# Nine selections beside the chunked phases, stores from GpSimd's own queue, and shorter rings of K and V

## The chip, the cores and the metric

The kernel runs on one core of one Trainium2 chip. The metric is the device time of one execution in microseconds (us). A core has five engines that each take their instructions in order: TensorE (PE in the profile; PEld are its weight loads), VectorE (DVE), ScalarE (ACT), GpSimd (POOL) and SyncE (SP), which issues most DMA transfers.

## The reference, cut to what matters

Two blocks follow each other on 2048 tokens of width 1024, in float32. The first (sliding-window attention, a gated recurrence, a mixture of experts) is not touched. The second is:

```
xn   = rms_norm(h, gain);  proj = xn @ w_in
qa, ka, va, ga, qb, kb, vb, gb, iq, ik, iw, za, zb = split(proj)
ya = chunked_relpos_attention(qa, ka, va, rel_bias) * silu(ga)
yb = dsa_sparse_attention(rope(qb), rope(kb), vb, rope(iq), rope(ik), iw) * silu(gb)
merged = sigmoid(za + b0) * (ya @ w_branch_a) + sigmoid(zb + b1) * (yb @ w_branch_b)
out = rms_norm(h + merged @ w_out, final_gain)
```

In the chunked attention, each chunk of 64 queries sees its own 64 keys and the 512 before them, in 8 heads of 64. In the sparse attention, each block of 128 queries (16 blocks) first selects keys: 8 index heads of 32 give `score = sum_h relu(iq_h . ik) * iw_h` over all keys up to the block's end, and each query keeps the 256 keys of highest score. Softmax attention of 8 heads with one shared key and value head of 64 then runs over the kept keys.

## The kernel before, in words

The second block is class `S3`. Products that need full precision are done as three products of a high and a low part (`mm3`); the parts have names ending in h and l, or `whi`, `wlo`.

**Who sets the order.** The program is written by generators ("lanes") that a small planner interleaves (`B.run`). Each lane yields until the engine that it wants, and its operands, are ready by the planner's own clock (`Clock`, `Engine.cost`); then its instruction is written down. Front lanes come first; the lane in `back` (named `fill`) gets an engine only when no front lane wants it. The result is a fixed order for each engine, which the chip follows; waits are semaphores.

**The phases** (`run`, from L2858 on):

- *Norms.* `norm_lane` gathers expert results (`cy`, by indirect DMA from GpSimd), adds (`cx`), normalises, transposes. `proj(0, ...)` begins the projections of the first 1024 tokens (half 0). `ev_n` copies a result out of PSUM; queries of the sparse part and of the index are rotated on GpSimd (`rotate`) and stored by SP to DRAM tensors QB and IQ.
- *Chunked phase 0* (`chunked(0, ...)`): 32 units `a_unit(p, c, t)`, for a pair of heads p and a block of 128 queries. K and V come in blocks of 256 tokens through a ring of `KR` = 6 blocks (`k_lane`); a unit uses three of them. Scores `pS<-K,Q`, bias and maximum on VectorE (`sc`), exponential on ScalarE, division by the sum on GpSimd (`softmax`: `sc<-sc,ast`), transposes `pT<-ident,sc` on PE, split (`split_p`, `pp`), products `pU<-pp,V`. Then GpSimd multiplies by the gate (`gate`: `ot<-ot,sg`), and the product is stored to YT by SP. The rest of the projections of half 0 and the start of half 1 is the `fill`.
- *Sparse phase 0* (`sparse(range(SPLIT), ...)`, SPLIT = 10): blocks 0 to 9. For each block `sel_unit` makes the selection: 8 index heads by pieces of 512 keys (`pS<-ikS,iqs`), relu on ScalarE (`rl<-pS`), accumulation on VectorE (`acc<-rl,iw,acc`), then `search`: 12 steps of bisection for the threshold, each a pass of ScalarE over the row (`bias<-acc,sst`) and two tiny ones (`sst<-sst`), and some passes of VectorE. The result is a row of biases, 0 or a large negative number (`bias`). Then 4 units `b_unit(blk, p)` do the attention: scores `pS<-kbS,qd`, `scb`, transposes `pT<-ident,scb`, products `pU<-pp,vbS`, gate, store to YT.
- *Chunked phase 1* with the last projections of half 1 as fill, then the rest of them.
- *Sparse phase 1*: blocks 10 to 15, with `tail(c)` as fill: for each 256 tokens the branch projections (`pA<-yt,..`, `pA<-yh,..`), the merge gates (`tz`), the output projection (`pA<-..,mh`, `pA<-..,ml`), the final norm. `tail(c)` loads YT of blocks 2c and 2c + 1, all heads, so it can start only when their sparse units are done; the last, `tail(7)`, needs block 15. ScalarE and VectorE split what it loads (`yh<-yt`, `yt<-yt,yh`).

`bias_load` and the DRAM tensor BIAS exist already: a selection in `stored` writes its row there, and a sparse phase loads it in place of making it. Before, nothing was stored. In `chunked`, `sel` sets how many buffers there are:

```
self.P, self.nrb, self.nsel, self.nrl, self.npp = P, 1 if sel else 2, 1, 1 if sel else 2, 2 if half and sel else 3
self.NM = (max(sel, default=0) + 1) * 128
self.stored.update(sel)
```

Of the kernel before, what the change touches and what calls it, by code (L numbers as in the profile page):

```python
# [103 lines left out]
class Engine:  # L104
# [11 lines left out]
    def __getattr__(self, f):  # L116
        real = getattr(self.eng, f)
        if not callable(real) or f in ("preload_act_table_set",):
            return real

        def call(*a, **k):
            r = real(*a, **k)  # L122
            out = k.get("out", a[0] if a else None)
            if is_ap(out):
                outs = [out] + [k[x] for x in ("accum_out",) if is_ap(k.get(x))]
                ins = [x for x in a[0 if "out" in k else 1:] if is_ap(x)]
                ins += [x for y, x in k.items() if y not in ("out", "accum_out") and is_ap(x)]
                ins += [x.ap for x in k.values() if hasattr(x, "ap") and not is_ap(x) and is_ap(x.ap)]
                cost, lat = self.cost(f, out, ins, k, [x for x in a + tuple(k.values()) if isinstance(x, AF)])
                self.clock.op(self.name, outs, ins, cost, lat, 1.46 if f == "indirect_dma_start" else 0.0)  # L130
            return r
        return call

    def cost(self, f, out, ins, k, fs):
        n = out.free_size()
        if f in ("dma_start", "indirect_dma_start"):
            b = out.size() * 4 if callable(out.size) else out.size * 4
            return (1.04, 0.0) if f != "dma_start" else (b / 3.6e5, 0.0)
        if self.name == "tensor":
# [1714 lines left out]
SPLIT = 10  # L1854
KR = 6


class S3:
# [190 lines left out]

    def store(self, dst, t, src=None, key=None):  # L2050

        b = self.b
        yield from b.on("sync", t)
        self.nc.sync.dma_start(dst, t.bitcast(F32) if src is None else src)
        b.done(t)
# [4 lines left out]
    def ev_n(self, g, blk, ps):  # L2060
# [14 lines left out]
        elif g:  # L2075
# [13 lines left out]
            yield 1  # L2089
            yield from self.store(dst, x, x.rearrange("p h d -> p (h d)"), key)  # L2090
        else:
# [109 lines left out]
    def k_lane(self, half):  # L2201

        b, nc, P, c = self.b, self.nc, self.P, self.b.clock
        self.K = P.tile([128, 2, 256 * KR], F32R, name="K", bufs=1)
# [50 lines left out]
    def a_unit(self, p, c, t):  # L2255
# [10 lines left out]
        place = lambda kt: ring[(blk - 4 + kt) // 2][0] * 2 + (blk + kt) % 2  # L2266
        r0, end = place(kts[0]) * 128, 256 * KR
        q_ = slice(t * 128, t * 128 + 128)
# [127 lines left out]
    def gate(self, ot, g, i, blk):  # L2396
# [3 lines left out]
        b.done(g)  # L2400
        yield from self.store(self.YT[i, :, blk * 128:blk * 128 + 128], ot, None, ("y", i, blk))

# [438 lines left out]
    def run(self):  # L2841
# [18 lines left out]
        with self.b.pool("s_k") as c:  # L2860
            self.consts(c)
            self.keys(c)
            with ExitStack() as st:
                en = lambda name: st.enter_context(b.pool(name))
                b.nld = 1
                self.XN, self.ld, Wp, self.st = en("s_xn"), en("s_ld"), en("s_w"), en("s_st")
                self.W = Weights(b, self.ld, Wp, srcs, ring=3, ahead=1, store=self.parts, keep=dict(enumerate(order)))
                b.lanes = [self.weight_lane()]
                with b.pool("s_ro") as c:
                    self.rope = c.tile([128, NTB, 24], F32, name="rope")  # L2870
                    with b.pool("s_c") as self.C:
# [7 lines left out]
                    self.W.hi_eng = "gpsimd"  # L2879
                    self.chunked(0, fill, ())  # L2880
                    self.sparse(range(SPLIT), fill)
                    self.go(fill)
                fill = chain(self.keep(), self.proj(1, range(12, 32), last=True))
                self.chunked(1, fill, ())
                self.go(fill)
# [54 lines left out]
    def chunked(self, half, fill, sel):  # L2940

        with self.b.pool("s_a") as P:
            self.P, self.nrb, self.nsel, self.nrl, self.npp = P, 1 if sel else 2, 1, 1 if sel else 2, 2 if half and sel else 3
            self.NM = (max(sel, default=0) + 1) * 128
# [150 lines left out]
```

## Time and profile before

| what | value |
|---|---|
| median of 3 runs | 4131.68 us (4124.09 to 4132.37) |
| profiled execution, its own time | 4132.75 us |
| its span, first to last instruction | 4131.0 us |
| mean granted TensorE clock | 0.944 of full speed |
| busy share of the span: PE / VectorE / ScalarE / GpSimd | 89 / 66 / 55 / 19% |
| second block in that span | from about 1645 us to the end |
| chunked phase 0 / sparse phase 0 / chunked phase 1 / tails and sparse phase 1 begin at about | 2018 / 2330 / 2957 / 3304 us |

Durations are from the profiled execution. An engine's busy time leaves out waits; PE's matmuls overlap, so 100% busy says that one follows another without a gap, and the granted clock says at which of its two levels (1.2 or 2.4 GHz) they ran. "Idle before, releaser" names what ended an engine's wait.

### The profile page before, as it was taken

The page shows a single profiled execution, that of the slowest core. Times are in us where ns is not written, and L with a number is a line of the kernel's source. Part 1 is how long each engine was busy: PE and PEld are TensorE (multiplying, and loading weights), DVE is VectorE, ACT ScalarE, POOL GpSimd, SP SyncE. Part 2 cuts the span into 40 slices and gives each one's busy share as a digit, 9 for nine tenths or more (in the row PEclk, how much of TensorE's full clock was granted, in tenths as well). Part 3 has the DMA queues.
Part 4 walks back from the last instruction along what each step waited for, and adds up shares of the span by engine and source line. Part 5 has one row for each costly group of instructions (what it writes and reads, how often), then busy time and mean ns, then how long its engine had stood idle before and what let it go on. Part 6 is the DMA issues. An engine that isn't in the chain of part 4 may idle for free.

```text
span 4131.0 us, 64766 instructions
## 1 busy us (share of the span) xinstructions
PE 3675.2 (89%) x21649; PEld 3189.6 (77%) x21649; DVE 2738.2 (66%) x7027; ACT 2265.0 (55%) x4628; POOL 788.6 (19%) x1474
## 2 busy tenths in 40 slices
PE   3999999979969998488899989999799979999796
PEld 2888788768858887487788879988588868988686
DVE  7866875688877776744356556775566148888772
ACT  3644654555546665433234468874355248767851
POOL 1310000131011110561144324100133111111000
PEclk9999999979989999699999989999799989999897
DMA  6232441134368886768888753443466398876155
GB/s 222 80 115 98 161 168 72 54 116 148 123 235 316 317 307 242 265 233 303 258 267 265 225 191 102 130 129 130 122 177 171 111 305 292 308 264 232 48 180 186
DMA packets 442096, 792.24 MB, mean 192 GB/s; under 512 B 129072, under 2 KB 267280, under 8 KB 440848
## 3 DMA queue, kind: packets, MB, share of 16 engines
q1 hardware_dynamic: 430224, 754.35, 54.1%
q0 software_dynamic: 11520, 33.57, 2.5%
q8 instruction: 176, 2.88, 0.3%
q14 instruction: 176, 1.44, 0.1%
HBM read 566.50 MB, written 229.65 MB: 193 GB/s over the span
## 4 chain that ended last, share of the span: by engine, by line
PE 35%; DMA 6%; DVE 5%; issue 4%; ACT 2%; SPq 1%; POOL 1%; DVEq 0%; POOLq 0%; ACTq 0%
PE pA L122 22%; PE pS L122 5%; PE pT L122 4%; PE pU L122 4%; DMA tz<-TZ 2%; DMA x<-IQ 1%; SPq L122 1%; DVE acc L122 1%; DVE pp L122 1%; DVE scb L122 1%; DMA x<-QB 0%; ACT bias L122 0%; ACT pp L122 0%; DMA V<-VA 0%; DMA Q<-QA 0%
## 5 line engine op out<-in xcount | busy, mean ns | idle before, releaser
L122 PE MATMUL pA<-xnl,whi 128*128 128x512 f32 x1024 | 412.8, 403 | 0.0
L122 DVE TENSOR_TENSOR wlo<-ld,whi 128x1024 fp32r<-128x1024 f32 x271 | 327.1, 1237 | 114.2 <-ACT whi L122 56.6
L122 PE MATMUL pA<-xnh,whi 128*128 128x512 f32 x1024 | 402.2, 393 | 0.0
L122 PE MATMUL pA<-xnh,wlo 128*128 128x512 f32 x1024 | 401.9, 392 | 0.0
L122 DVE TENSOR_TENSOR pp<-pT,pp 128x256 fp32r<-128x256 f32 (+1 forms) x568 | 296.5, 539 | 134.3 <-ACT pp L122 129.7
L122 ACT ACTIVATE pp<-pT 128x256 fp32r<-128x256 f32 (+1 forms) x568 | 261.1, 478 | 226.5 <-PE pT L122 214.7
L122 PE MATMUL pA<-hlo,whi 128*128 128x512 f32 x832 | 352.4, 424 | 10.0 <-issue 6.6
L122 PE MATMUL pA<-hhi,wlo 128*128 128x512 f32 x832 | 329.7, 396 | 0.0
L122 PE MATMUL pA<-hhi,whi 128*128 128x512 f32 x832 | 328.8, 395 | 0.0
L122 ACT ACTIVATE whi<-ld 128x1024 fp32r<-128x1024 f32 x212 | 213.2, 1052 | 50.4 <-PE pA L122 35.0
L122 DVE SCALAR_TENSOR_TENSOR acc<-rl,iw,acc 128x512 f32<-128x512 f32 (+3 forms) x304 | 213.6, 703 | 37.0 <-ACT rl L122 24.0
L122 PE MATMUL pU<-pp,vbS 128*128 128x256 f32 x1088 | 212.7, 309 | 21.3 <-DVE pp L122 13.5
L122 PEld LDWEIGHTS pA<-xnh,wlo 128*128 128x128 f32 x1024 | 193.1, 189 | 42.8
L122 PE MATMUL pA<-wlo,xnh 128*128 128x256 f32 (+1 forms) x672 | 203.8, 303 | 25.1 <-DMA xnh<-XND 6.8
L122 ACT ACTIVATE bias<-acc,sst 128x384 f32<-128x384 f32 (+13 forms) x168 | 219.8, 1309 | 8.7 <-DVE sst L122 6.2
L122 PEld LDWEIGHTS pA<-xnl,whi 128*128 128x128 f32 x1024 | 194.0, 189 | 30.8
L122 PEld LDWEIGHTS pA<-xnh,whi 128*128 128x128 f32 x1024 | 193.8, 189 | 30.6
L122 PE MATMUL pA<-whi,xnl 128*128 128x256 f32 (+1 forms) x672 | 198.9, 296 | 4.0 <-DMA xnl<-XND 4.0
L122 PE MATMUL pA<-whi,xnh 128*128 128x256 f32 (+1 forms) x672 | 198.9, 296 | 0.0
L122 PEld LDWEIGHTS pU<-pp,vbS 128*128 128x128 f32 x1088 | 165.5, 199 | 37.5 <-DVE pp L122 21.2
L122 PE MATMUL pS<-kbS,qd 128*128 128x512 f32 (+3 forms) x640 | 183.0, 385 | 9.9 <-DVE bst L122 6.6
L122 ACT ACTIVATE rl<-pS 128x512 f32<-128x512 f32 (+3 forms) x304 | 159.3, 542 | 58.0 <-PE pS L122 29.7
(491 smaller groups left out, 10917.4 us busy)
## 6 DMA issues: line engine op xcount, KB each, us to landing
whi<-W2P SPq DMA_DIRECT2D x172, 512.0 KB
wlo<-W2P SPq DMA_DIRECT2D x172, 512.0 KB
ld<-in_w_gu_dram SPq DMA_DIRECT2D x128, 512.0 KB
ld<-in_w_dn_dram SPq DMA_DIRECT2D x64, 512.0 KB
W2P<-whi SPq DMA_DIRECT2D x57, 512.0 KB
W2P<-wlo SPq DMA_DIRECT2D x57, 512.0 KB
Y<-ym SPq DMA_DIRECT2D x48, 512.0 KB
xl<-in_wadaT_dram SPq DMA_DIRECT2D x32, 512.0 KB
```

The lines of the kernel that those rows point to most:

```text
L122: r = real(*a, **k)
```

## The change

1. The selections of blocks 2 to 7 run as a front lane beside chunked phase 0, those of blocks 10 to 12 beside chunked phase 1. Their bias rows go to BIAS, and the sparse phases load them. Blocks 0, 1, 8, 9 and 13 to 15 stay where they were. With selections beside it, a chunked phase has one `rl`, one `acc`, 4 in place of 5 rows `sc`, and in half 1 two products `pp` in place of three.
2. Stores of what GpSimd has written last (YT after the gate, QB and IQ after the rotation) are issued by GpSimd's queue instead of SP's: 128 + 32 + 16. The planner counts 1.04 us of GpSimd for one, and the bytes on the DMA engines.
3. The ring of K and V has 4 blocks in half 0 and 5 in half 1, instead of 6. The buffer into which raw weights are loaded lies in a pool that ends with sparse phase 0.

```diff
@@ Engine.__getattr__, Engine.cost @@
-                self.clock.op(self.name, outs, ins, cost, lat, 1.46 if f == "indirect_dma_start" else 0.0)
+                far = 1.46 if f == "indirect_dma_start" else out.size() * 4 / 3.6e5 if f == "dma_start" and self.name != "sync" else 0.0
+                self.clock.op(self.name, outs, ins, cost, lat, far)
...
-            return (1.04, 0.0) if f != "dma_start" else (b / 3.6e5, 0.0)
+            return (1.04, 0.0) if f != "dma_start" or self.name != "sync" else (b / 3.6e5, 0.0)
@@ S3 @@
-KR = 6
...
-    def store(self, dst, t, src=None, key=None):
+    def store(self, dst, t, src=None, key=None, eng="sync"):
...
-        yield from b.on("sync", t)
-        self.nc.sync.dma_start(dst, t.bitcast(F32) if src is None else src)
+        yield from b.on(eng, t)
+        getattr(self.nc, eng).dma_start(dst, t.bitcast(F32) if src is None else src)
@@ ev_n @@
-            yield from self.store(dst, x, x.rearrange("p h d -> p (h d)"), key)
+            yield from self.store(dst, x, x.rearrange("p h d -> p (h d)"), key, "gpsimd")
@@ gate @@
-        yield from self.store(self.YT[i, :, blk * 128:blk * 128 + 128], ot, None, ("y", i, blk))
+        yield from self.store(self.YT[i, :, blk * 128:blk * 128 + 128], ot, None, ("y", i, blk), "gpsimd")
@@ run @@
-                self.XN, self.ld, Wp, self.st = en("s_xn"), en("s_ld"), en("s_w"), en("s_st")
-                self.W = Weights(b, self.ld, Wp, srcs, ring=3, ahead=1, store=self.parts, keep=dict(enumerate(order)))
-                b.lanes = [self.weight_lane()]
+                self.XN, Wp, self.st = en("s_xn"), en("s_w"), en("s_st")
+
                 with b.pool("s_ro") as c:
+                    self.W = Weights(b, c, Wp, srcs, ring=3, ahead=1, store=self.parts, keep=dict(enumerate(order)))
+                    b.lanes = [self.weight_lane()]
...
-                    self.chunked(0, fill, ())
+
+                    self.chunked(0, fill, range(2, 8))
...
-                self.chunked(1, fill, ())
+                self.chunked(1, fill, range(SPLIT, SPLIT + 3))
@@ chunked @@
-            self.P, self.nrb, self.nsel, self.nrl, self.npp = P, 1 if sel else 2, 1, 1 if sel else 2, 2 if half and sel else 3
+            self.KR = 4 + half
+            self.P, self.nrb, self.nsel, self.nrl, self.npp = P, 2, 1, 1 if sel else 2, 2 if half and sel else 3
```

The order of the instructions moves at three places. On PE, at the end of sparse phase 1, around the last product of block 15 (`pU<-pp,vbS`; tiles carry the number that the program gave them), the kernel before has:

```order
L122 MATMUL pT_45846<-ident,scb_45546 128x128
L122 MATMUL pU_45752<-pp_45840,vbS 128x256 x4
L122 MATMUL pU_45752<-pp_45851,vbS 128x256 x2
L122 MATMUL pU_45752<-ident,rr_45859 128x128
L122 MATMUL pU_45752<-pp_45851,vbS 128x256 x2
L122 MATMUL pA_45885<-yt_45876,whi_45312 128x256
L122 MATMUL pA_45885<-yh_45878,whi_45312 128x256
```

The last product is followed at once by `tail(7)`, which reads `yt`. In the changed kernel the last product stands here:

```order
L122 MATMUL pA_45528<-yh_44277,wlo_45245 128x256
L122 MATMUL pU_45418<-pp_45561,vbS 128x256 x4
L122 MATMUL pU_45418<-pp_45571,vbS 128x256 x2
L122 MATMUL pU_45418<-ident,rr_45591 128x128
L122 MATMUL pU_45418<-pp_45571,vbS 128x256 x2
L122 MATMUL pA_45606<-wlo_45349,mh_44855 128x256
L122 MATMUL pA_45606<-whi_45348,mh_44855 128x256
L122 MATMUL pA_45606<-whi_45348,ml_44856 128x256
```

What follows is `tail(6)` (`mh`, `ml`): 223 matmuls of it stand between block 15 and the first of `tail(7)`. Farther up, between `tail(5)` and `tail(6)`, the kernel before has 216 rows without a tail, and the changed one nowhere more than 26.

On SP, at the switch into chunked phase 1, ahead of the first K and V blocks, the kernel before has:

```order
L122 DMA sg_33093<-SG 128x128
L122 DMA YT<-ot_33111 128x128
L122 DMA YT<-ot_33168 128x128
L2218 DMA K<-KA 64x2x256 x2
L2220 DMA V<-VA 128x2x256
```

and the changed kernel:

```order
L122 DMA sg_32906<-SG 128x128
L122 DMA sg_33013<-SG 128x128
L122 DMA sg_33108<-SG 128x128
L2218 DMA K<-KA 64x2x256 x2
L2220 DMA V<-VA 128x2x256
```

The two stores to YT that stood ahead of the loads are gone from SP; 5 blocks in place of 6 are then loaded ahead of Q.

On GpSimd, in chunked phase 1, the changed kernel has the stores between the steps of the units (`sc<-sc,ast` is the division by the sum, `ot<-up` and `ot<-ot,sg` a unit's result and its gate):

```order
L122 DMA YT<-ot_36188 128x128
L122 TENSOR_SCALAR sc_36128<-sc_36128,ast 128x640
L122 TENSOR_TENSOR ot_36310<-up_36266 64x128 x2
L122 TENSOR_SCALAR sc_36239<-sc_36239,ast 128x640
L122 TENSOR_SCALAR sc_36247<-sc_36247,ast 128x640
L122 TENSOR_TENSOR ot_36310<-ot_36310,sg_36346 128x128
L122 DMA YT<-ot_36310 128x128
```

The kernel before has the same steps without the rows `DMA YT<-ot`; a store now follows each gate and stands ahead of the next division.

## Rows read from the trace of the kernel before

**Rows 1.** Busy time in stretches: us of each engine (instructions), granted clock, DMA.

```profile
core 0: us, PE busy (x) PEld busy (x) DVE busy (x) ACT busy (x) POOL busy (x), PEclk, DMA share, GB/s
1645.00:1925.00 280.00, 187.45 (x1346) 180.43 (x1347) 158.54 (x329) 116.78 (x242) 146.55 (x304) 0.80 0.75 263
1925.00:2018.00 93.00, 93.00 (x412) 77.01 (x411) 22.27 (x27) 19.49 (x27) 1.06 (x1) 1.00 0.80 266
2600.00:2650.00 50.00, 48.58 (x389) 47.06 (x388) 33.71 (x86) 47.13 (x114) 3.73 (x9) 1.00 0.33 113
2878.00:2936.00 58.00, 47.88 (x263) 38.17 (x261) 38.27 (x104) 28.66 (x49) 2.81 (x8) 0.85 0.15 43
2957.00:3240.00 283.00, 276.88 (x1574) 241.71 (x1574) 166.27 (x584) 145.95 (x348) 95.39 (x168) 0.97 0.57 169
3240.00:3304.00 64.00, 64.00 (x284) 52.93 (x282) 0.00 (x0) 7.57 (x11) 0.00 (x0) 1.00 0.33 115
3304.00:3319.00 15.00, 1.53 (x7) 0.83 (x5) 2.98 (x2) 3.19 (x3) 0.00 (x0) 0.65 0.88 287
3400.00:3800.00 400.00, 384.37 (x2864) 360.02 (x2864) 336.67 (x829) 303.00 (x551) 61.72 (x89) 0.99 0.84 284
3800.00:3903.00 103.00, 71.44 (x348) 54.93 (x347) 81.64 (x205) 84.70 (x138) 4.08 (x11) 0.82 0.14 47
```

**Rows 2.** Timeline, end of the second sparse phase: start us, duration us, engine, instruction.

```profile
4040.37 0.48 PE L122 MATMUL pU<-pp,vbS 128*128 128x256 f32 x2
...
4042.82 0.32 SPq L122 DMA_DIRECT2D YT<-ot  x1
...
4049.87 1.91 ACT L122 ACTIVATE yh<-yt 128x2048 fp32r<-128x2048 f32 x1 [8.60 <-DMA yt<-YT]
...
4054.16 0.58 PE L122 MATMUL pA<-yt,whi 128*128 128x256 f32 x1 [13.30 <-DVE yt L122]
...
4054.97 0.41 PE L122 MATMUL pA<-yt,whi 128*128 128x256 f32 x1
...
4055.18 0.41 PE L122 MATMUL pA<-yh,whi 128*128 128x256 f32 x1
...
4059.82 0.28 PE L122 MATMUL pA<-yt,whi 128*128 128x256 f32 x1
...
4059.94 0.28 PE L122 MATMUL pA<-yh,whi 128*128 128x256 f32 x1
```

**Rows 3.** Timeline, switch from sparse phase 0 to chunked phase 1.

```profile
2929.98 8.16 SPq L122 DMA_DIRECT2D YT<-ot  x2
...
2938.25 1.24 SPq L2218 DMA_DIRECT2D K<-KA  x2
...
2949.82 1.24 SPq L122 DMA_DIRECT2D Q<-QA  x2
...
2956.80 1.40 PE L122 MATMUL pS<-K,Q 128*128 128x320 f32 x4 [20.94 <-DMA Q<-QA]
```

**Rows 4.** Groups of ScalarE by shape, 3300 to 3720: busy us, mean ns, idle before.

```profile
L122 ACT ACTIVATE rl<-pS 128x512 f32<-128x512 f32 x112 | 63.8, 593 | 20.0 <-DVE acc L122 9.7 <-PE pS L122 9.6 <-PE pA L122 0.3
...
L122 ACT ACTIVATE bias<-acc,sst 128x1536 f32<-128x1536 f32 x12 | 18.9, 1576 | 0.2
...
L122 ACT ACTIVATE sst<-sst,wd 128x1 f32<-128x1 f32 x42 | 16.1, 384 | 0.7
...
L122 ACT ACTIVATE sst<-sst 128x1 f32<-128x1 f32 x42 | 12.3, 293 | 0.2
...
L122 ACT ACTIVATION_READ_ACCUMULATOR bias<-acc,sst 128x1 f32 x42 | 7.9, 187 | 0.0
```

**Rows 5.** Instructions on tile Y, GpSimd's gathers: ns min/median/max.

```profile
L122 POOL DMA_INDIRECT cy<-Y,pos x32: 984/998/1762, 1649.1 to 1869.4; - x32
```

**Rows 6.** Timeline of GpSimd, two gathers in a row.

```profile
1650.43 0.99 POOL L122 DMA_INDIRECT cy<-Y,pos  x1 [0.30 <-issue]
```

**Rows 7.** Waits of PE, 1925 to 2330: us in total, times, longest us.

```profile
PE pT L122 <- POOL sc L122: 9.5, 6, 4.8
```

More of the change, by code (lines that the diff above doesn't have):

```diff
@@ L2201, in k_lane @@
     def k_lane(self, half):
-        b, nc, P, c = self.b, self.nc, self.P, self.b.clock
+        b, nc, P, c, KR = self.b, self.nc, self.P, self.b.clock, self.KR
         self.K = P.tile([128, 2, 256 * KR], F32R, name="K", bufs=1)
@@ L2266, in a_unit @@
         place = lambda kt: ring[(blk - 4 + kt) // 2][0] * 2 + (blk + kt) % 2
-        r0, end = place(kts[0]) * 128, 256 * KR
+        r0, end = place(kts[0]) * 128, 256 * self.KR
         q_ = slice(t * 128, t * 128 + 128)
```

## Prediction

> **What bounds the kernel now.** The page comes first: TensorE (PE) is busy for 89% of the span, VectorE 66%, ScalarE 55%, GpSimd 19%. The PE rows of a call are the same before and after this change, only their order differs. So the question is where PE stands still or runs at the lower granted clock, and whether the new order fills those places. The second view is the busy time in stretches [rows 1]. Each of its rows gives a stretch, PE's busy time with the number of matmuls, the other engines, and the granted clock. Four things are to be seen there.
>
> First, most stretches of the second block are full: 384.37 of 400 us from 3400 to 3800, 276.88 of 283 from 2957 to 3240 (chunked phase of half 1), 64.00 of 64 from 3240 to 3304, where nothing but projections is left. Second, there is a hole in the second sparse phase. From 3800 to 3903 PE does 348 matmuls in 103 us, where it did 2864 in 400 us just before, and the clock drops to 0.82. VectorE is busy for 81.64 us and ScalarE for 84.70 us. This is the stretch in which the tails have run out (the order shows 216 rows without one), so that the chain of the last sparse blocks and their selections is all PE has. Third, the end of that phase: the last matmul of block 15 starts at 4040.37 and the next one, of the last tail, at 4054.16, 13.30 us idle [rows 2]. Between them lie the store to YT, the load of it, 1.91 us of ScalarE and the split on VectorE. Fourth, the switch from the first sparse phase to chunked phase 1: 58 us with 263 matmuls only (no projection left to fill), then 20.94 us in which PE waits for the load of Q [rows 1, 3].
>
> **The sum.** It is made against the profiled execution's own time of 4132.75 us (span 4131.0); the median of the runs shown, 4131.68, is 1.1 us lower, and that is taken off at the end. A measurement of this kernel can tell about 0.2% (8 us) from no change.
>
> 1. *Selections of blocks 10 to 12 leave the second sparse phase.* Twelve search steps of block 11 take 12 x (1.576 + 0.187 + 0.293 + 0.384) = 29.3 us of ScalarE, its 24 score pieces 24 x 0.593 = 14.2 us [rows 4]; with the three blocks about 3 x 45 = 135 us of ScalarE go from a phase where it was the busiest engine beside PE. The sparse units of these blocks can start at once, so they spread evenly among the tails: in the new order no stretch without a tail is longer than 26 rows. At the mixed stretch's rate, 400/2864 = 0.140 us a matmul, the 348 matmuls would take 48.6 us in place of 103 [rows 1]. **-54.4 us.** The low bound is the idle time alone, 103 - 71.44 = 31.6 us, as the hole's matmuls are larger on average than a tail's; I take the upper figure since the clock comes back too (0.82 to 0.99).
>
> 2. *The end of the phase.* In the new order 223 matmuls of tail 6 stand between block 15's last product and the last tail. Matmuls of that shape follow each other every 0.12 us at the full clock, the pair at 4059.82 [rows 2], so they last 27 us, twice the 13.3 us chain. The last tail then does not start cold either: after the gap its matmuls come every 0.21 us [rows 2], the pair at 4054.97, the lower of the two clock levels (1.2 against 2.4 GHz); from 4054.16 to 4059.82 that makes some 27 matmuls at 0.09 us lost, 2.4 us. **-15.7 us**, bounds -13.3 and -15.7. If the store from GpSimd lands some us later, the cover of 27 us still holds it.
>
> 3. *Stores issued by GpSimd, and the switch into chunked phase 1.* 176 stores (128 of YT, 48 of QB and IQ) leave SP's queue. At the switch SP stands 8.16 us at two YT stores that wait for GpSimd's products, and only then issues the loads of K, V and Q [rows 3]; behind them 18 loads stand before Q, now 15 (the ring has 5 blocks, 0.6 us per issue by the row of two K loads in 1.24 us: 1.9 us). How early K can start is set by when block 9's tiles are read for the last time, which is when PE's idle time begins, at about 2936 (2956.80 - 20.94), so at most 2 us are free before K from that side and 8 from the other. **-6 us**, bounds 0 and -10. Elsewhere the stores free 176 x 0.32 us [rows 2] of SP, which is hidden: SP does not bound.
> The Trainium skill, DMA: Bandwidth & Descriptors, section "Issuing engines are not separate DMA queues", says that issuing from several engines saves only the sequencer's issue time, since all run on the same 16 DMA engines. By that rule this term would be the three issues alone, -2 us. The trace differs at this one place: what is saved is not issue time but a wait of 8.16 us that stood ahead of other loads.
> On GpSimd each store costs an issue. No row shows a plain store from GpSimd; the nearest is its gather, 0.998 us in the median, 1.762 at most, with 0.30 between two of them [rows 5, 6], so 1.3 us each; below, SP's 0.32. That is 64 x 1.3 = 83 us in the two chunked phases, where GpSimd is busy 95.39 of 283 us [rows 1]: hidden, **0**, with the price if not under the rivals. In the norm stage (1645 to 1925) 24 stores add 31 us to GpSimd's 146.55 of 280; the new order lets PE do projections there that it did from 1925 to 2018 (93.00 us with GpSimd at 1.06), so a late norm is covered: 0, bounds -15 and +15, the latter being half of the 31 us.
>
> 4. *Selections of blocks 2 to 7 go beside chunked phase 0.* The chunk units end with many projections left, so the selections' tail has cover. But projections used there are missing later: between the last projection and block 9's last product the order now has 410 matmuls, before 257. They ran at 58/263 = 0.221 us each, against 0.140 mixed [rows 1]: 153 x 0.081 = **+12 us**, bounds 0 and 153 x 0.221 = 34.
>
> 5. *Selections of 10 to 12 go beside chunked phase 1.* ScalarE then does 145.95 + 7.57 + 135 = 289 us in 283 + 64 us plus 80 moved matmuls of 512 columns at 64/284 = 0.23 us (18 us), 79%. From 2600 to 2650 ScalarE was busy for 47.13 of 50 us and PE still for 48.58 [rows 1]. The 64 us of pure projections become mixed, at 97% instead of 100%: 2 us, and one buffer less for scores and products; **+5 us**, bounds 0 and 20. The rings of 4 and 5 blocks leave one or two blocks ahead of a window of three; a late block delays chunk units, and PE does projections meanwhile: 0.
>
> 6. *The switch to the tails* was idle for 13.5 of 15 us (3304 to 3319) [rows 1]. Four search steps of block 12 (2.44 us each, 9.8 us) now stand on ScalarE behind the last projection's copy and ahead of the split that the first tail waits for. Part of it passes while YT loads: **+5 us**, bounds 0 and 25 (all of it, and the end of the search on VectorE).
>
> Stores and loads of nine bias blocks go beside everything at DMA shares of 0.57 and 0.84: 0.
>
> Sum: -54.4 - 15.7 - 6 + 12 + 5 + 5 = -54; 4132.75 - 54 = 4078.7, less 1.1: **4078 us**.
>
> **Rivals.** *GpSimd's queue binds: slower.* Each of the 64 chunk units has its rows scaled on GpSimd before PE may transpose them, and the previous unit's store now stands ahead of that scaling. If PE waits out the 1.3 us in every unit, 64 x 1.3 = 83 us come back: 4161. It decides from 54/64 = 0.84 us a unit. For it: PE waited for this scaling already, 9.5 us in 6 times around phase 0 [rows 7]; PE takes its rows in order. Against it: that is 6 waits in 32 units, GpSimd is idle two thirds of the time, and the planner already counts 1.04 us for a store there. The Trainium skill, SBUF — State Buffer, section "SBUF: two separate sides", warns that a DMA issued from GpSimd is held up while VectorE holds the port pair they share in its faster modes. By that rule a store would cost more than its issue. The trace agrees at most in size: the gathers spread from 0.984 to 1.762 us beside a working VectorE [rows 5]. Chance 0.10.
>
> *The chunked phases give it back: no change.* The 135 us of ScalarE's selection work stand in one queue with the chunk units' exponentials and copies. If a third of it falls on PE's rows, 45 us return: 4123, from 4110 to 4140. For: PE's order is fixed, and real steps that come late stop it. Against: 2600 to 2650, above. Chance 0.12.
>
> *More than forecast.* The terms of +12, +5 and +5 vanish since lighter sparse blocks run faster than those of rows 1, and the norm stage, where PE is idle 92.5 of 280 us, gains 15 with SP's queue free: 4041. Chance 0.12.
>
> **How the numbers follow.** The forecast case has 0.65, anything else 0.01. Faster: 0.65 + 0.12 + 0.05 of the give-back = 0.82; same: 0.05 of it and the rest, 0.06; slower: 0.10 and 0.02, 0.12. The range goes from 4037 (terms 1 and 2, -10, nothing lost, -15 in the norm stage) to 4128, the middle of the give-back; beyond lie the slower rival and half of the give-back, some 0.16.
>
> **What would show it.** Right: no stretch of 50 us in the second sparse phase with PE under 45; no gap of over 3 us ahead of the last tail; PE's wait for Q at the switch shorter than 21 us; 410 matmuls without projections over about 90 us at the end of the first sparse phase; PE's waits for GpSimd's scaling under 30 us in both chunked phases together. Wrong: those waits at 80 us; ScalarE over 90% with PE under 90% in chunked phase 1; a new gap where the tails begin of more than 40 us.

## The result, and the profile after

| kernel | median us (range, runs) | ratio to the kernel before, 95% interval |
|---|---|---|
| before | 4132.02 (4124.09 to 4140.01, 4) | 1 |
| changed | 4058.22 (4054.27 to 4061.26, 4) | 0.9822 [0.9807, 0.9836] |

The change makes the kernel 74 us faster; 54 were forecast (4078, range 4037 to 4128). The profiled execution took 4061.26 us, with a span of 4059.4 us against 4131.0, and a mean granted clock of 0.951 against 0.944. The busy time in stretches of the changed kernel, with the columns of [rows 1]:

```profile
core 0: us, PE busy (x) PEld busy (x) DVE busy (x) ACT busy (x) POOL busy (x), PEclk, DMA share, GB/s
1645.00:1925.00 280.00, 193.09 (x1371) 185.31 (x1372) 145.74 (x309) 112.14 (x231) 151.73 (x327) 0.81 0.71 253
...
2854.00:2955.00 101.00, 78.58 (x424) 60.83 (x422) 70.71 (x201) 61.34 (x112) 10.64 (x24) 0.86 0.18 53
2961.00:3240.00 279.00, 274.10 (x1470) 231.51 (x1470) 188.60 (x561) 201.74 (x436) 101.94 (x163) 0.97 0.61 178
3240.00:3332.00 92.00, 89.82 (x492) 76.94 (x490) 54.65 (x166) 66.63 (x143) 30.77 (x53) 1.00 0.29 98
3332.00:3366.00 34.00, 1.56 (x6) 1.17 (x7) 11.23 (x12) 12.90 (x20) 0.00 (x0) 0.57 0.45 159
...
3400.00:3800.00 400.00, 390.30 (x2969) 371.96 (x2968) 335.53 (x857) 285.04 (x483) 68.84 (x101) 0.99 0.78 266
3800.00:3903.00 103.00, 99.87 (x771) 95.90 (x770) 76.89 (x195) 59.35 (x93) 13.01 (x20) 0.98 0.70 246
```

The last row stands where the hole of before was: 771 matmuls in 103 us instead of 348, at 0.98 instead of 0.82. The row 2854 to 2955 is the end of sparse phase 0 without a projection, now 101 us long instead of 58. The row 3332 to 3366 is the switch to the tails: 34 us with 1.56 us of PE, where before it was 15.

The end of sparse phase 1 in the timeline of the changed kernel (start us, duration us, engine, instruction, idle before), which answers to [rows 2]:

```profile
3958.34 0.49 PE L122 MATMUL pU<-pp,vbS 128*128 128x256 f32 x2
...
3961.13 0.58 POOL L122 DMA_DIRECT2D YT<-ot  x1 [0.29 <-POOL ot L122]
...
3963.70 0.37 SPq L122 DMA_DIRECT2D yt<-YT  x1
...
3970.89 1.91 ACT L122 ACTIVATE yh<-yt 128x2048 fp32r<-128x2048 f32 x1 [11.19 <-DMA yt<-YT]
...
3972.83 2.29 DVE L122 TENSOR_TENSOR yt<-yt,yh 128x2048 fp32r<-128x2048 f32 x1 [1.70 <-ACT yh L122]
...
3982.16 0.28 PE L122 MATMUL pA<-yt,whi 128*128 128x256 f32 x1
```

The chain from block 15's last product to the split `yt` ends at 3975.12, and the first matmul of the last tail follows at 3982.16 without a gap: tail 6 covers the chain with 7 us to spare.

The switch into chunked phase 1, in the timelines of SP and PE, against [rows 3]:

```profile
2943.35 1.24 SPq L2218 DMA_DIRECT2D K<-KA  x2
...
2952.95 1.23 SPq L122 DMA_DIRECT2D Q<-QA  x2
...
2954.39 0.48 PE L122 MATMUL pU<-pp,vbS 128*128 128x256 f32 x2
2960.68 1.40 PE L122 MATMUL pS<-K,Q 128*128 128x320 f32 x4 [5.80 <-DMA x<-IQ]
```

The loads of K begin 11 us before PE's last product of block 9. PE stands for 5.80 us; before, for 20.94.

The switch to the tails, timelines of ScalarE, VectorE, SP and PE:

```profile
3340.28 1.68 ACT L122 ACTIVATE bias<-acc,sst 128x1664 f32<-128x1664 f32 x1
...
3349.14 1.95 DVE L122 SCALAR_TENSOR_TENSOR bias<-acc,sst,big 128x1664 f32<-128x1664 f32 x1
...
3351.13 0.32 SPq L122 DMA_DIRECT2D BIAS<-bias  x1
3351.54 0.38 SPq L122 DMA_DIRECT2D fg<-in_fgain_dram  x1
3352.22 2.41 SPq L122 DMA_DIRECT2D x<-QB  x4
3354.87 0.36 SPq L122 DMA_DIRECT2D yt<-YT  x1
...
3357.97 1.09 PE L122 MATMUL pT<-ident,x 128*128 128x128 f32 x4 [26.39 <-DMA x<-QB]
3365.52 0.58 PE L122 MATMUL pA<-yt,whi 128*128 128x256 f32 x1 [6.46 <-DVE yt L122]
```

This is the new gap of the change. PE's wait is put down to the load of `x`, but the load goes out late: ahead of it in SP's queue stands the store of block 12's row, and that waits for the last pass of the search (ScalarE's last step at 3340.28, VectorE's last pass at 3349.14).

The marks of both timelines, made into a balance against the steps of the sum (us; spans, so 4131.0 to 4059.4; each column is one execution, and those of the changed kernel lie up to 7 us apart):

| stretch | before | after | difference | forecast |
|---|---|---|---|---|
| up to the first chunk score | 2026.5 | 2024.5 | -2 | 0 |
| from there to sparse phase 0's last product | 909.4 | 930.4 | +21 | +12 |
| switch into chunked phase 1 | 20.9 | 5.8 | -15 | -6 |
| from there to the last projection | 347.5 | 370.9 | +23 | +23 (5, and 18 of moved matmuls) |
| switch to the tails | 14.6 | 33.9 | +19 | +5 |
| from the first tail to the end | 812.1 | 693.9 | -118 | -88 (70, and 18 moved away) |
| sum | 4131.0 | 4059.4 | -72 | -54 |

### The profile page after: what moved, and what is told of

Same layout as the page of the kernel before. It is cut to its first block, busy times and chain, and to the rows that moved or that the text cites. A ratio compares the mean times of both kernels' runs of the same rounds, so it can differ in the third digit from the quotient of the medians.

```text
span 4059.4 us, 64576 instructions
## 1 busy us (share of the span) xinstructions
PE 3646.1 (90%) x21649; PEld 3167.4 (78%) x21649; DVE 2734.8 (67%) x7027; ACT 2283.2 (56%) x4628; POOL 901.4 (22%) x1650
## 4 chain that ended last, share of the span: by engine, by line
PE 37%; DMA 7%; POOL 4%; DVE 3%; issue 3%; ACT 2%; SPq 1%; POOLq 0%; DVEq 0%; ACTq 0%
PE pA L122 22%; PE pS L122 5%; PE pT L122 5%; PE pU L122 5%; POOL rot L122 1%; DMA x<-IQ 1%; SPq L122 1%; DMA x<-QB 1%; DMA tz<-TZ 1%; POOL st L122 1%; DMA Q<-QA 0%; DMA sg<-SG 0%; DVE scb L122 0%; DVE pp L122 0%; POOL QB L122 0%
## 5 line engine op out<-in xcount | busy, mean ns | idle before, releaser
L122 DVE SCALAR_TENSOR_TENSOR acc<-rl,iw,acc 128x512 f32<-128x512 f32 (+3 forms) x304 | 220.8, 727 | 38.0 <-ACT rl L122 31.4
L122 ACT ACTIVATE bias<-acc,sst 128x1152 f32<-128x1152 f32 (+13 forms) x168 | 220.0, 1309 | 13.3 <-DVE sst L122 9.6
L122 PE MATMUL pU<-pp,vbS 128*128 128x256 f32 x1088 | 203.2, 301 | 10.2 <-DVE pp L122 8.3
L122 ACT ACTIVATE st<-pA 128x256 f32<-128x256 f32 (+4 forms) x160 | 73.6, 460 | 202.6 <-PE pA L122 161.5
L122 PEld LDWEIGHTS pA<-hlo,whi 128*128 128x128 f32 x832 | 159.4, 192 | 35.9 <-issue 9.4
```

## The experiments

Twelve kernels were run, each beside runs of the kernel before on the same chip. All compute the whole result.

| label | median us | ratio to before, 95% interval |
|---|---|---|
| stores_only | 4109.5 | 0.9947 [0.993, 0.9963] |
| stores_on_sp | 4136.32 | 1.0009 [0.9999, 1.0019] |
| late_three_only | 4057.01 | 0.983 [0.981, 0.985] |
| early_six_only | 4141.71 | 1.0018 [1.0006, 1.003] |
| order_kept_issue_sp | 4086.57 | 0.9883 [0.9867, 0.99] |
| order_of_sp_issue_gp | 4122.89 | 0.9971 [0.9957, 0.9985] |
| search_first | 4106.2 | 0.9935 [0.9918, 0.9953] |
| late_three_search_first | 4093.01 | 0.9905 [0.9889, 0.9922] |
| bias_store_gp | 4053.5 | 0.9803 [0.9781, 0.9825] |
| late_three_bias_gp | 4042.87 | 0.9783 [0.9758, 0.9807] |
| gp_stores_twice | 4343.53 | 1.0497 [1.0469, 1.0525] |
| gp_stores_halves | 4080.05 | 0.9863 [0.9844, 0.9882] |

### One part of the change at a time

**stores_only**: no selection moved.

```diff
-                    self.chunked(0, fill, range(2, 8))
+                    self.chunked(0, fill, ())
...
-                self.chunked(1, fill, range(SPLIT, SPLIT + 3))
+                self.chunked(1, fill, ())
```

> No selection is moved; the stores from GpSimd and the rings of 4 and 5 blocks stay. My theory: the gain of the change (74 us) comes from blocks 10 to 12, whose selections left the second sparse phase, so here the hole before the last tails and the 13 us gap ahead of the last tail are back; only the switch into chunked phase 1 is shorter (by up to 15 us): 4115, from 4105 to 4130. Rival (GpSimd's own queue is what pays, since SP no longer stands at stores): 4080 or less.

4109.5 us. As expected from the theory, and near its faster end: the hole is still there (96.62 us of PE in the 120 us from 3780 to 3900), PE waits 13.96 us ahead of the last tail, and the time from the first tail to the end is 799 us, where the changed kernel takes 694. The rings of 4 and 5 blocks are in this kernel too, as in all the others, so its 23 us belong to the stores, the rings and the order planned for both; no run parts the rings from the rest.

**stores_on_sp**: the selections moved, the stores left where they were.

```diff
-            yield from self.store(dst, x, x.rearrange("p h d -> p (h d)"), key, "gpsimd")
+            yield from self.store(dst, x, x.rearrange("p h d -> p (h d)"), key)
...
-        yield from self.store(self.YT[i, :, blk * 128:blk * 128 + 128], ot, None, ("y", i, blk), "gpsimd")
+        yield from self.store(self.YT[i, :, blk * 128:blk * 128 + 128], ot, None, ("y", i, blk))
```

> Selections as in the change, all stores back on SP. My theory: nearly all of the gain stays, and the switch into chunked phase 1 goes back from 6 us of idle PE to about 20: 4072, from 4058 to 4085. Rival (GpSimd's queue pays): 4110 or more. Second rival (the 176 stores cost GpSimd's chain in the chunked phases something): 4050 or less.

4136.32 us: the theory fell. The selections alone gain nothing. Yet the second sparse phase did what it was to do: from the first tail to the end it takes 717 us, 95 less than before. What was gained there is lost ahead of it: the first tail comes 99 us later than in the kernel before. Against the changed kernel, chunked phase 1 begins at 3007.9 instead of 2960.7, its projections end 55 us later, and the second sparse phase is 23 us longer. The trace of this kernel shows one place where much of it arises, in stretches, in ScalarE's groups by shape from 2876 to 2900, and in PE's timeline:

```profile
2860.40:2988.90 128.50, 84.97 (x492) 67.11 (x490) 84.49 (x238) 90.50 (x175) 6.54 (x20) 0.87 0.10 28
2878.10:2899.30 21.20, 0.04 (x1) 0.04 (x1) 7.53 (x15) 20.85 (x47) 0.46 (x1) 0.62 0.00 0
```

```profile
L122 ACT ACTIVATE bias<-acc,sst 128x1280 f32<-128x1280 f32 x9 | 12.2, 1357 | 0.1
L122 ACT ACTIVATE bias<-acc,sst 128x1152 f32<-128x1152 f32 x4 | 5.0, 1246 | 0.0
...
L122 ACT ACTIVATE upb<-pU 64x256 f32<-64x256 f32 x1 | 0.4, 380 | 0.0
```

```profile
2899.26 0.69 PE L122 MATMUL pS<-kbS,qd 128*128 128x128 f32 x2 [21.16 <-DVE bst L122]
```

The searches of blocks 8 (1152 keys) and 9 (1280 keys) run alternately on ScalarE, at 98% busy, and PE has no projection left. In the changed kernel the same two searches run from 2794 to 2881, mostly beside projections, which last until 2854.9. That is a matter of the order that the planner wrote, and the order here is another one. So this run mixes two things, the queue and the order. The next two part them.

**late_three_only** and **early_six_only**: one half of the selections each.

```diff
-                    self.chunked(0, fill, range(2, 8))
+                    self.chunked(0, fill, ())
```

> Only blocks 10 to 12 are selected beside chunked phase 1, blocks 2 to 7 are again in the first sparse phase. My theory: the changed kernel ended the first sparse phase 19 us later than the kernel before because projections were used up beside the early selections; without them that end comes back to about 2936 us and the whole gains some 20 more: 4040, from 4030 to 4052. Rival (the early selections are worth something, or the shorter ring made that delay): 4058 or more.

4057.01 us, where 4040 was expected: a miss in the total. The first half of the reason held, since sparse phase 0 ends at 2933.1 and chunked phase 1 starts 22 us earlier than in the changed kernel (7 of these are there at the first chunk score already). But from the first tail to the end it takes 704 us instead of 694, and the switch to the tails is 1 us longer; the profiled execution (span 4049.3) is 10 us ahead of the changed kernel's, the median 1 us, since the one was the fastest of its four and the other the slowest. The early six are worth nothing measurable here; why the last phase is 10 us longer stays open.

```diff
-                self.chunked(1, fill, range(SPLIT, SPLIT + 3))
+                self.chunked(1, fill, ())
```

> Only blocks 2 to 7 are selected early, beside chunked phase 0; blocks 10 to 12 are in the second sparse phase again. My theory: the hole and the gap ahead of the last tail come back, the first sparse phase ends 19 us later, the switch stays short: 4135, from 4120 to 4150, no faster than before by more than 12. Rival (the early selections carry part of the gain): 4110 or less.

4141.71 us, as the theory expected. Without the late three, the early six cost 32 us against stores_only.

Where each part acts can be read from the marks of the PE timelines (us, one execution each):

| stretch | before | stores_only | late_three_only | changed | stores_on_sp |
|---|---|---|---|---|---|
| up to sparse phase 0's last product | 2935.9 | 2943.9 | 2933.1 | 2954.9 | 2988.9 |
| switch into chunked phase 1 | 20.9 | 5.4 | 6.0 | 5.8 | 19.0 |
| from there to the last projection | 347.5 | 348.1 | 370.6 | 370.9 | 378.9 |
| switch to the tails | 14.6 | 15.7 | 35.1 | 33.9 | 31.4 |
| from the first tail to the end | 812.1 | 799.2 | 704.4 | 693.9 | 716.9 |

Up to the switch, stores_only and late_three_only have the same order of instructions on PE, VectorE, ScalarE and GpSimd; their 11 us of difference in the first row are noise. The late three act in the last three rows: +22, +19 and -95, which is 53 us, and the medians of these two kernels differ by 52.

### The order and the queue

**order_kept_issue_sp** uses the planner's order for stores on GpSimd, but issues them from SP. PE's instructions stand in the changed kernel's order.

```diff
             setattr(self, e, Engine(e, getattr(nc, e), clock))
+        self.asp = Engine("gpsimd", nc.sync, clock)
...
-        getattr(self.nc, eng).dma_start(dst, t.bitcast(F32) if src is None else src)
+        (self.nc.asp if eng == "gpsimd" else self.nc.sync).dma_start(dst, t.bitcast(F32) if src is None else src)
```

> The changed kernel in the order of its own plan on TensorE, VectorE, ScalarE and GpSimd; only the 176 stores are issued by SP, each at the place in the program where GpSimd would have issued it. It separates what the stores on SP lost (78 us) into queue and order. Theory A (order: with stores on SP the planner writes another order, whose first sparse phase ends in two searches side by side with a 21 us hole): most of the gain stays, and only SP's waits ahead of the switches come back, some 20 us: 4078, from 4062 to 4095. Theory B (queue: loads stand behind stores that wait for GpSimd all through the chunked phases): 4110 or more.

**order_of_sp_issue_gp** is the reverse.

```diff
+        self.agp = Engine("sync", nc.gpsimd, clock)
...
-        yield from b.on(eng, t)
-        getattr(self.nc, eng).dma_start(dst, t.bitcast(F32) if src is None else src)
+        yield from b.on("sync", t)
+        (self.nc.agp if eng == "gpsimd" else self.nc.sync).dma_start(dst, t.bitcast(F32) if src is None else src)
```

> The reverse: the order that the planner writes for stores on SP, but the 176 stores issued by GpSimd at those places. Theory A (order): the hole of 21 us at the end of the first sparse phase stays, the switch into chunked phase 1 is short again: 4115, from 4100 to 4130. Theory B (queue): 4085 or less.

The four medians, with all nine selections moved:

| order planned for stores on | issued by GpSimd | issued by SP | queue |
|---|---|---|---|
| GpSimd | 4058.2 | 4086.6 | 28 |
| SP | 4122.9 | 4136.3 | 13 |
| order | 65 | 50 | |

Theory A held in both. Of the 78 us between the changed kernel and stores_on_sp, the order is worth 50 to 65 and the queue 13 to 28. Between order_of_sp_issue_gp and the changed kernel, where the queue is the same, 42 of the 65 us lie ahead of sparse phase 0's last product and the rest behind the switch. In the second kernel the hole is there again, 21.16 us at 2906.65, and the wait at the switch is 5.31 us. In the first, half of the queue's price lies at one place, the switch into chunked phase 1 (timelines of SP and PE of order_kept_issue_sp):

```profile
2954.28 8.17 SPq L122 DMA_DIRECT2D YT<-ot  x2
2962.55 1.23 SPq L2219 DMA_DIRECT2D K<-KA  x2
...
2979.69 1.40 PE L122 MATMUL pS<-K,Q 128*128 128x320 f32 x4 [19.52 <-DMA Q<-QA]
```

SP stands 8.17 us at two stores, as it did before [rows 3], and K goes out after PE's last product at 2959.68 instead of 11 us ahead of it. PE's wait grows from 5.80 to 19.52 us. Of the other 13 us between the two spans, 5 lie ahead of the switch and 8 behind it.

### The gap ahead of the tails

**search_first** puts the lane of selections ahead of the chunk units in chunked phase 1; **late_three_search_first** does that to late_three_only.

```diff
-            self.go(pipe(self.a_units(half), 4), self.k_lane(half), self.a_loads(half), self.rb_lane(half), self.sel_lane(sel), back=(fill,))
+            self.go(*([self.sel_lane(sel)] if half else []), pipe(self.a_units(half), 4), self.k_lane(half), self.a_loads(half), self.rb_lane(half), *([] if half else [self.sel_lane(sel)]), back=(fill,))
```

> The changed kernel with the lane of selections ahead of the chunk units in chunked phase 1, so that the planner serves it first; the bias row of block 12 is then stored 24 SP instructions ahead of the first tail load instead of just before it. Theory (the 26 us gap ahead of the first tail is the search of block 12, behind whose store SP holds the tail's loads): the gap falls to under 14 us, the time to 4042, from 4030 to 4052. Rival (chunk units then wait for ScalarE and give it back in the phase): 4054 or more.

> Only blocks 10 to 12 selected early, with their lane ahead of the chunk units. Theory: the early end of the first sparse phase (2933 instead of 2955 us) and the short switch to the tails add up: 4030, from 4015 to 4045. Rival (a phase that ends early only meets a later wait, as late_three_only at 4057 suggests): 4050 or more.

4106.2 and 4093.01 us, 48 and 36 us slower than without the edit. The gap fell as expected, from 26.39 to 12.36 us. But the times are on the side of the two rivals, though not by their mechanism. In stretches of search_first:

```profile
2967.00:3294.00 327.00, 321.64 (x1640) 270.13 (x1640) 188.72 (x529) 225.41 (x471) 85.08 (x142) 0.98 0.51 160
3294.00:3395.00 101.00, 66.02 (x319) 50.93 (x319) 64.33 (x207) 50.57 (x124) 40.70 (x70) 0.77 0.34 100
```

The projections are used up at 3294, and the chunk units that were put off run alone until 3395: 319 matmuls in 101 us at a clock of 0.77. Until 3294 PE is at 98%, so the chunk units did not hold it up by waiting for ScalarE; what was spent is the cover. The same happens at the end of sparse phase 0 in the changed kernel, with the early six.

**bias_store_gp** keeps the changed kernel's order and lets GpSimd issue the nine stores to BIAS; **late_three_bias_gp** does it in the order of late_three_only, with three.

```diff
+        self.agp = Engine("sync", nc.gpsimd, clock)
...
-        getattr(self.nc, eng).dma_start(dst, t.bitcast(F32) if src is None else src)
+        (self.nc.agp if key and key[0] == "bs" else getattr(self.nc, eng)).dma_start(dst, t.bitcast(F32) if src is None else src)
```

> The changed kernel in its own order, only the nine stores of the selections' rows to BIAS issued by GpSimd instead of SP. Theory (the 26 us gap ahead of the first tail is SP standing at the store of block 12's row, with the loads of fg, x and YT behind it): the loads go out some 15 us earlier, the gap falls under 14 us: 4044, from 4032 to 4052. Rival (the tail's buffers lie where the search's rows lie, so the loads wait for the end of the search whoever stores it): gap as before, 4054 to 4064.

> Only blocks 10 to 12 selected early (the order of late_three_only), their three rows stored to BIAS by GpSimd. Theory (SP standing at the last of them holds the tail's loads): 4042, from 4030 to 4050, 15 us under late_three_only. Rival (buffers, not the queue): 4050 to 4062.

4053.5 us, between the two expectations, and 4042.87 us, as the theory had it. The timelines of SP, PE and VectorE of bias_store_gp:

```profile
3338.09 1.91 SPq L122 DMA_DIRECT2D x<-QB  x4
...
3343.39 1.09 PE L122 MATMUL pT<-ident,x 128*128 128x128 f32 x4 [7.14 <-DMA x<-QB]
...
3347.68 1.95 DVE L122 TENSOR_SCALAR_CACHE_REDUCE bias<-acc,sst 128x1664 f32<-128x1664 f32 x1
...
3357.16 2.28 DVE L122 TENSOR_TENSOR yt<-yt,yh 128x2048 fp32r<-128x2048 f32 x1
...
3359.49 0.58 PE L122 MATMUL pA<-yt,whi 128*128 128x256 f32 x1 [15.02 <-DVE yt L122]
```

The load of `x` goes out 14 us earlier, while the search still runs, so the buffers did not hold it: it was the queue. But the gap falls by 11 us only (26.39 + 6.46 to 7.14 + 15.02), as the next thing in line is VectorE, where the passes of block 12's search, from 3347.68 on, stand ahead of the split `yt`. The median falls by 5 us, within the spread of the two kernels' executions. In the order of late_three_only the same edit is worth 14 us, and there all four executions (4036 to 4050) lie below those without it (4051 to 4068). late_three_bias_gp is the fastest of all, at 0.9783 [0.9758, 0.9807]; it beats the kernel before by 92 us and the changed one by 15 in the median, with intervals that meet at 0.9807.

### What a store costs GpSimd

**gp_stores_twice** and **gp_stores_halves** keep the changed kernel's order and double GpSimd's issues.

```diff
         getattr(self.nc, eng).dma_start(dst, t.bitcast(F32) if src is None else src)
+        if eng == "gpsimd":
+            self.nc._nc.gpsimd.dma_start(dst, t.bitcast(F32) if src is None else src)
```

> The changed kernel in its own order, but each of the 176 stores that GpSimd issues is issued twice in a row, the same bytes to the same place. The prediction's term of 0 for GpSimd's queue: hidden, 4058 to 4068. Its slower rival (each store stands ahead of the next unit's scaling and TensorE waits it out): 64 times 0.88 us in the chunked phases alone, 56 us: 4105 or more.

4343.53 us: neither. The second store of a pair writes where the first does, and in this program it waits for the semaphore of the first's landing. GpSimd's groups, from 1640 us to the end (busy us, mean ns, idle before):

```profile
L2056 POOL DMA_DIRECT2D YT<-ot x128 | 69.4, 542 | 405.8 <-DMA YT<-ot 355.3 <-DVE ast L122 18.3 <-DVE pp L122 9.7
...
L2056 POOL DMA_DIRECT2D QB<-st x32 | 17.4, 542 | 75.9 <-DMA QB<-st 70.3 <-issue 5.6
...
L2056 POOL DMA_DIRECT2D IQ<-st x16 | 8.7, 544 | 37.6 <-DMA IQ<-st 37.6
```

The second issues keep GpSimd for 95.5 us and leave it idle for 519.3. Of these 615 us, 285 come out as time. So a GpSimd that is busy for 22% of the span, as in the changed kernel, is not a queue with room to spare: what stands in it is waited for.

```diff
+class NoIssue:
+    def dma_start(self, *a):
+        pass
...
+        self.count = Engine("gpsimd", NoIssue(), clock)
...
+            for r in (slice(0, 64), slice(64, 128)):
+                self.nc._nc.gpsimd.dma_start(dst[r], v[r])
+            self.nc.count.dma_start(dst, v)
```

> The changed kernel in its own order, each of the 176 stores issued by GpSimd as two halves of 64 partitions, so that no second issue waits for the first to land as it did in gp_stores_twice (3.2 us between two issues there, and 285 us in all). It prices the issue alone: 0.54 to 0.58 us more of GpSimd per store. The prediction's term of 0: hidden, 4058 to 4066. Its slower rival at the measured price, one wait of 0.55 us in each of 64 chunk units and in 24 stores of the norm stage, or in all 176: 4100 to 4160. Between: a part of the issues stands on the path.

4080.05 us, the case between: 22 us more than the changed kernel. GpSimd's groups of this kernel:

```profile
L2063 POOL DMA_DIRECT2D YT<-ot x256 | 141.1, 553 | 43.5 <-POOL ot L122 34.2 <-issue 6.5 <-DVE bst L122 2.8
...
L2063 POOL DMA_DIRECT2D QB<-st x64 | 34.9, 548 | 9.3 <-POOL st L122 9.1
L2063 POOL DMA_DIRECT2D IQ<-st x32 | 17.6, 553 | 4.7 <-POOL st L122 4.7
```

Together they take 193.6 us; the 176 issues of the changed kernel take 102.6 (74.6, 18.6 and 9.4 us, from 1640 us to the end). Of the 91 us more, 22, or 24%, come out as time. The run also doubles the number of transfers, so not all of the 22 need come from the issues.

## Why the prediction was right, and which of its steps were not

The total was right, and the main reason too, but three steps failed and two terms were mis-sized, with opposite signs. That the total came within 20 us is in part luck: by the balance above, terms 1 to 3 brought 39 us more than forecast, terms 4 and 6 took 23 more. Of the signs that were to show it, three held: no gap ahead of the last tail, 5.80 us at the switch, and short waits for the scaling. The matmuls without projections took 10 us longer than forecast, and one stretch of 50 us (3625.5 to 3675.5) has PE busy for 44.35 us, just below 45.

**Terms 1 and 2 (-70): right, and 30 less than came.** The hole is filled, the end is covered, and stores_on_sp shows both (717 us for the phase) without the stores on GpSimd. In the last row of the table of stretches 118 us went, where 88 were forecast (70, and 18 of moved matmuls). Of them the late three bring 95 (stores_only to late_three_only), 7 more than forecast. Another 13 are there in stores_only, with no selection moved, and 10 come only with the early six; the sum had neither in this phase. The whole stretch from the first tail to block 15's last product (kernel before, changed kernel, stores_on_sp) shows that the gain is not in the hole alone:

```profile
3319.00:4041.00 722.00, 653.41 (x4652) 601.42 (x4652) 566.44 (x1390) 501.83 (x877) 88.47 (x137) 0.95 0.68 229
```

```profile
3366.00:3959.00 593.00, 575.35 (x4359) 549.22 (x4359) 468.92 (x1200) 379.79 (x636) 95.50 (x144) 0.98 0.77 262
```

```profile
3418.18:4021.30 603.12, 573.54 (x4304) 542.40 (x4305) 464.18 (x1195) 379.52 (x634) 78.06 (x118) 0.98 0.74 252
```

Outside the hole the kernel before did 4304 matmuls in 619 us, 0.144 each; the changed one does 4359 in 593, 0.136. Its ScalarE has 122 us less to do in the phase, but so has that of stores_on_sp, at 0.140. So the lighter ScalarE goes with half of the faster rate at most; what makes the other half is not shown.

**Term 3 (stores on GpSimd, -6): the step on K failed.** It said that how early K can start is set by the last reading of block 9's tiles, when PE's idle time begins, so that at most 2 us were free, bounds 0 and -10. In the changed kernel K starts 11 us before that product, so the tiles did not hold it. What held it were the two stores: order_kept_issue_sp, with the same order on the other four engines, brings them back and with them a wait of 19.52 us. The switch gained 15 us, outside the bounds. That elsewhere the stores on SP cost nothing (hidden, as SP does not bound) failed too: in the same order the queue is worth 28 us, some 14 of it at this switch. The Trainium skill, DMA: Bandwidth & Descriptors, section "Issuing engines are not separate DMA queues", would have had the issues' time alone; and its section "Issuing engine by pattern" gives simple stores to Sync. Here the measurement goes the other way: in one order, 4058.2 us from GpSimd and 4086.6 from SP. What is saved at the switch is not issue time but a wait of SP.

**The price on GpSimd (hidden, 0): failed in the small.** A store takes 0.58 us, and 0.29 before it, not the 1.3 of the estimate (GpSimd's groups of the changed kernel from 2018 to 3330, then PE's waits for the scaling in the two chunked phases):

```profile
L122 POOL DMA_DIRECT2D YT<-ot x104 | 60.6, 583 | 33.6 <-POOL ot L122 24.8 <-DVE sst L122 2.9 <-issue 2.9
...
L122 POOL DMA_DIRECT2D QB<-st x16 | 9.3, 580 | 4.7 <-POOL st L122 4.7
```

```profile
PE pT L122 <- POOL sc L122: 12.7, 7, 4.1
...
PE pT L122 <- POOL sc L122: 3.1, 3, 1.8
```

PE's waits for GpSimd's scaling are 15.8 us in both phases together, under the 30 that were allowed, so the slower rival did not come. But gp_stores_halves shows that an issue is not free either: at most 0.125 us of time for each more. The 28 us are what is left after that price. The hold-up that the Trainium skill describes for DMAs from GpSimd (SBUF — State Buffer, section "SBUF: two separate sides") does not show in the issues: all 128 to YT take between 578 and 628 ns beside a working VectorE. Whether VectorE was in such a mode at those moments no view tells.

**Term 4 (+12): too small.** The 410 matmuls without projections took 100 us instead of about 90, and sparse phase 0's last product came 21 us later, counted from the first chunk score, within the bounds of 0 and 34. The early selections are the cause of most of it: this stretch takes 930 us with them, and 920 (stores_only) and 915 (late_three_only) without. The other 6 to 11 us above the 909 of the kernel before came with the stores, the rings and their order, for which the sum had nothing here.

**Term 5 (+5): right.** With the 18 us of moved matmuls 23 were forecast, and 23 measured; ScalarE is busy 268 of 371 us (201.74 + 66.63), 72% where 79% were estimated, and PE 98%. The rival by which the chunked phases give the gain back had its price paid in sum (21 + 5 + 19 = 45 us), but at the ends of the phases, not inside them, and more than forecast came back elsewhere.

**Term 6 (+5): the step "part of it passes while YT loads" failed.** The four search steps of block 12 behind the last projection were right. But the load of YT stood behind the store of that search's result in SP's queue, so nothing passed beside it, and VectorE's passes at the end of the search, 8 us from 3343.03 on, which stood in the bound but not in the sum, came on top: +19 us, within the bounds of 0 and 25. bias_store_gp shows the queue's share, 11 us of the gap.

**What no step had:** the order, and that the parts need each other. The sum added the stores' -6 to the selections' -48. Run apart, the nine selections give nothing (4136.3), the stores with the rings 23 us (4109.5); together they give 74. Most of this is the order: pricing a store on GpSimd instead of SP makes the planner write another order on all engines, and with the nine selections that is worth 50 to 65 us by itself.

The table of stretches shows which selections need it. Behind sparse phase 0's last product the selections gain with the stores on either queue: 49 us there in stores_on_sp, against the kernel before, and 52 in the median from stores_only to late_three_only. Ahead of it, of the selections, only the early six act. With them that product comes 53 us later in stores_on_sp than in the kernel before, but only 11 to 22 later in the changed kernel than in stores_only and late_three_only. So it is mainly the early six that the order for stores on SP serves badly, and they bring nothing in the other. No run has the late three alone with the stores on SP. Why the one order came out better was seen at one place (the searches of blocks 8 and 9, 21 us) and is open for the rest.

## What to carry to other kernels

Where a planner sets the order, an edit is two edits, what the chip does and what the planner then writes. Run the new queue in the old order and the old queue in the new order before you name a cause: of the 78 us here, the queue had 28 and the order 50, or 13 and 65 when counted the other way round.

An in-order queue is priced by what stands behind its waits, not by its issue time. Ask of each store that waits for an engine which load is next, and who waits for that load. Here an engine at 22% busy returned up to a quarter of the issue time that was added to its queue.

Change one part at a time within a change: here the late three carry the gain, and the early six cost a little or much, as the order has it.

Work that fills gaps is a stock. Moving a serial search beside it saves the search's idle time once, and takes the cover from whatever comes last in that phase.

## What was not expected of the hardware

A plain store of 64 KB from GpSimd took it 0.58 us, less than the gather's 0.998 [rows 5], and landed 3.1 us after its issue in the median (1.9 to 8.1, over the 48 of 128 stores to YT whose landing the trace has). The stores to QB and IQ, 128 KB each, took 0.58 us too; a store of half the partitions took 0.55, with 32 KB as with 64. So between these sizes the issue does not follow the bytes. A second store to the same place, which this program lets wait for the first one's semaphore, cost GpSimd 2.95 us of idle time in the mean (519.3 us in 176), most of it until the first had landed.
